# A decoder layer's gate matrix build: slab eviction in runs of four tokens, and GpSimd's products on VectorE

## The chip, the cores and the metric

The kernel runs on one core of one Trainium2 chip. The metric is the device time of one execution in microseconds (us). The engines are named as the profile names them: PE is TensorE (PEld its weight loads), DVE is VectorE, ACT is ScalarE, POOL is GpSimd, SP is SyncE, which here only issues transfers. The five run side by side, each through its own queue of instructions in a fixed order, and wait for each other by semaphores. SBUF is the on-chip memory of 128 partitions, PSUM the memory into which PE writes its results.

## The reference

One decoder layer on 1024 tokens of width 1024: a layer norm, a mixer of eight attention heads with forget gates and four recurrent HGRN2 heads, an output projection, a second norm, and PEER channel mixing over 16384 single-neuron experts. The part around the change is PEER:

```python
q = (xt @ w_q).astype(F32).reshape(T, PEER_HEADS, 2, PEER_HALF)
s = jnp.einsum('thpd,hpnd->thpn', q, sub_keys.astype(F32))
s_top, i_top = lax.top_k(s, PEER_TOPK)
...
best, pos = lax.top_k(cand, PEER_TOPK)
idx = jnp.take_along_axis(cand_idx, pos, axis=-1)
gates = jax.nn.softmax(best, axis=-1)
...
    u = u_tab[idx_b]
    h = jax.nn.gelu(jnp.einsum('td,ted->te', x_b, u), approximate=False) * g_b
    return jnp.einsum('te,ted->td', h, v_tab[idx_b])
```

Each token picks 128 experts (8 heads, 16 each), an expert being a pair (i, j) of 128 by 128, with a gate each.

## The kernel before

The tokens are eight blocks of 128, worked in three groups (256, 512 and 256 tokens). Each group passes through projection, attention and recurrence (`fox`, `hgrn`), output projection with the second norm (`mix_out`), expert selection (`select`, 16 query projections with their top-16 searches on VectorE) and a selection tail.

Then PEER is computed in two ways. Blocks 0, 1, 6 and 7 (`GATHER`) fetch the expert rows of each token by indirect DMAs on GpSimd and multiply them up on VectorE. Blocks 2 to 5 (`DENSE`, 512 tokens) run through all 16384 experts by matrix products, the **dense stage**, which streams both expert tables from memory. For it each dense token needs its gates as a matrix over all experts. `gbuild` makes this **gate matrix**. It runs as a background job: `tick`, called from the loops of the last group's `mix_out` and `select`, lets it advance at set rates, and what is left is drained after `select`, before the dense stage.

How `gbuild` works. A block of 128 tokens goes in 16 groups of 8 tokens (`t8`). For each group four tiles of 128 x 1024 half-precision numbers are made (`per`, line 947; the 128 partitions are the 128 choices of a token, the 1024 columns 8 tokens by 128 values):

- `ohi`: 1 where the choice's i equals the column, always on VectorE; `ohj` the same for j;
- `ah` = `ohi` times the high half of the gate, `al` = `ohi` times its low half.

The constant `GBW` says for each of the four blocks, and for even and odd `t8`, which engine makes `ah`, `al` and `ohj`: `a` is ACT (eight instructions, line 958), `p` GpSimd, `v` VectorE. Tiles have two buffers each. For each token PE multiplies `ohj` by `ah` and by `al` (lines 972 and 974) and adds both in PSUM: 128 by 128 gates, j in the partitions, i in the columns. Four tokens fill one PSUM bank, `pt`, indexed [j, t, i]. ACT copies the bank, scaled, into the **slab** (line 977), a tile of 128 x 128 x 32 numbers indexed [j, i, t] that holds 32 tokens; after eight such evictions SyncE sends it out as 2 MB (line 980, `d_g`). There are 16 slabs and one slab buffer (`slabs = 1`), so the next eviction waits for the landing.

What else runs there, by the names in the rows: `wlo` is the low half of a weight tile, raw minus `whi`, on GpSimd in this stretch (line 213); `cand` are the sums that pairs of scores make (line 833), and `MAX8`, `FIND_INDEX8` and `MATCH_REPLACE8` the top-16 searches on VectorE; `dxt`, `dxh`, `dxl` are the dense tokens, loaded (line 999), transposed by PE and split into halves for the dense stage (lines 273 and 279); `rst`, `rsy`, `g` are tiny operations of norms and gates.

The order on each engine is made by a scheduler when the kernel is built, from the order of the code and estimates of its own; it differs from the order of the code where nothing forbids it.

Of the kernel before, what the change touches and what calls it, by code (L numbers as in the profile page):

```python
# [14 lines left out]
AF = mybir.ActivationFunctionType  # L15
# [43 lines left out]
W0 = 0.71  # L59
BANKS = {"h": 2, "v": 1, "f": 3}  # L60
AHEAD = {('fox', 512): 1, ('mix', 512): 1, ('sel', 512): 1}
GBW = (('apv', 'vvv'), ('apv', 'vvv'), ('apv', 'vvv'), ('vvv', 'vvv'))
LAG = 1
GATHER = (0, 1, 6, 7)
DENSE = (2, 3, 4, 5)
# [6 lines left out]
class Layer:  # L72
# [849 lines left out]
    def gbuild(self, blks, pool):  # L922
        nc, V = self.nc, self.nc.vector
        iota = pool.tile([P, P], F16, name="iota16h", tag="iota16h")
        nc.scalar.activation(iota, self.iota, AF.Copy)
        iv = iota.rearrange("p (m c) -> p m c", c=2).unsqueeze(1).to_broadcast([P, 8, 64, 2])

        def onehots():
            for blk in blks:
                sel = pool.tile([P, 3, P], F32, name="gsl", tag="gsl")  # L930
                nc.sync.dma_start(sel, self.d_sel[blk])
                gs, gh = (pool.tile([P, P], F32, name=n, tag=n, bufs=2) for n in ("gs_", "gh_"))
                g16 = pool.tile([P, P], F16, name="g16", tag="g16")
                pr = pool.tile([P, 4, P, 2], F16, name="gpair", tag="gpair", bufs=2)
                V.tensor_scalar(gs, sel[:, 2], GS, None, op0=ALU.mult)
                V.tensor_copy(g16, gs)
                V.tensor_copy(gh, g16)
                V.tensor_tensor(gs, gs, gh, op=ALU.subtract)
                for n, x in enumerate((sel[:, 0], sel[:, 1], gh, gs)):
                    nc.scalar.activation(pr[:, n], x.unsqueeze(2).to_broadcast([P, P, 2]), AF.Copy)  # L940
                for t8 in range(16):
                    t0 = t8 * 8

                    def per(name, x, n, op, eng=V):
                        t = pool.tile([P, 8, P], F16, name=name, tag=name, bufs=2)
                        y = pr[:, n, t0 : t0 + 8].unsqueeze(2).to_broadcast([P, 8, 64, 2])
                        eng.tensor_tensor(t.rearrange("p t (m c) -> p t m c", c=2), x, y, op=op)
                        return t

                    w = GBW[blks.index(blk)][t8 % 2]  # L950
                    ev = {"v": nc.vector, "p": nc.gpsimd}
                    oi = per("ohi", iv, 0, ALU.is_equal)
                    ov = oi.rearrange("p t (m c) -> p t m c", c=2)
                    oj = per("ohj", iv, 1, ALU.is_equal, ev[w[2]])
                    if w[0] == "a":
                        ah = pool.tile([P, 8, P], F16, name="ah", tag="ah", bufs=2)
                        for t in range(8):
                            nc.scalar.activation(ah[:, t], oi[:, t], AF.Copy, scale=gh[:, t0 + t : t0 + t + 1])
                    else:
                        ah = per("ah", ov, 2, ALU.mult, ev[w[0]])  # L960
                    al = per("al", ov, 3, ALU.mult, ev[w[1]])
                    yield blk, t8, oj, ah, al

        slab = [None]

        def build(blk, t8, oj, ah, al):
            if t8 % 4 == 0:
                slab[0] = pool.tile([P, P, 32], F32, name="slab", tag="slab", bufs=self.slabs)
            for t4 in range(0, 8, 4):
                pt = self.bank("h").rearrange("p (t i) -> p t i", t=4)  # L970
                for t in range(4):
                    nc.tensor.matmul(pt[:, t], oj[:, t4 + t], ah[:, t4 + t], start=True, stop=False,
                                     skip_group_check=True)
                    nc.tensor.matmul(pt[:, t], oj[:, t4 + t], al[:, t4 + t], start=False, stop=True,
                                     skip_group_check=True)
                c = t8 % 4 * 8 + t4
                nc.scalar.activation(slab[0][:, :, c : c + 4].rearrange("p i t -> p t i"), pt, AF.Copy,
                                     scale=1.0 / GS)
            if t8 % 4 == 3:
                self.q("dg").dma_start(self.d_g[DENSE.index(blk) * 4 + t8 // 4], slab[0])  # L980

        oh = onehots()
        cur = next(oh)
        yield 2
        while cur:
            build(*cur)
            cur = next(oh, None)
            yield 2
# [313 lines left out]
```

## Time and profile before

| | us |
|---|---|
| median of three runs (3123.66 to 3131.1) | 3125.99 |
| the profiled execution | 3124.38 |
| its span, first to last instruction | 3122.6 |
| busy in the span: PE / DVE / ACT / POOL | 2629.1 / 2728.4 / 1143.5 / 1725.8 |
| gate matrix build: first product to last landing | about 1242 to 1561 |
| slab evictions on ACT, 128 of them | 127.6 |
| dense stage | about 1561 to the end |

Read a busy time against its own stretch of the program: an engine that is half idle in the whole span can be the one that all others wait for in a part of it. A long mean duration is read against the shortest of the same operation: the difference is time in which the instruction had begun and did not get on. A wait is put down to the event that came last before it ended.

### The profile page before, as it was taken

How to read it: one execution, taken by the hardware profiler on the slowest of the kernel's cores; microseconds unless marked ns; L12 is line 12 of the kernel's file. 1: busy time of each engine (PE TensorE's matmuls, PEld its weight loads, DVE VectorE, ACT ScalarE, POOL GpSimd, SP SyncE). 2: the span in 40 equal slices, each digit the busy share in tenths (PEclk: the TensorE clock that was granted, in tenths of full speed). 3: DMA queues.
4: the chain of work that ended last, by engine and by line, in shares of the span. 5: the costliest groups of instructions: out<-in, count | busy, mean ns of one | idle time of the engine just before them, and what ended most of it. 6: DMA issues, size and time to landing. Idle time of an engine off the chain costs nothing. (4 is left out here: it accounts for less than half of the span.)

```text
span 3122.6 us, 45664 instructions
## 1 busy us (share of the span) xinstructions
PE 2629.1 (84%) x16057; PEld 2161.1 (69%) x16057; DVE 2728.4 (87%) x5549; ACT 1143.5 (37%) x2028; POOL 1725.8 (55%) x1264
## 2 busy tenths in 40 slices
PE   7767799777779767767459899899999999999995
PEld 6767689656657445657347778787778877877874
DVE  8658766588769988989889899899999999999998
ACT  4733222455222433776523223232222323322321
POOL 2343477555756644654036666665467665656652
PEclk9879899888889889878779999999999999999997
DMA  7542599755968857663379999999999999999994
GB/s 272 191 143 81 195 353 318 224 157 169 336 247 297 282 192 268 221 232 149 149 243 366 333 380 359 350 362 367 345 362 371 380 379 357 356 375 337 371 338 159
DMA packets 338662, 887.13 MB, mean 284 GB/s; under 512 B 29912, under 2 KB 124136, under 8 KB 336000
## 3 DMA queue, kind: packets, MB, share of 16 engines
q0 software_dynamic: 147456, 536.94, 47.1%
q1 hardware_dynamic: 185200, 338.38, 31.1%
q10 hardware_dynamic: 5776, 8.90, 0.8%
q8 instruction: 126, 2.06, 0.3%
q14 instruction: 104, 0.85, 0.1%
HBM read 821.67 MB, written 62.42 MB: 283 GB/s over the span
## 5 line engine op out<-in xcount | busy, mean ns | idle before, releaser
L1090 POOL DMA_INDIRECT rows<-in_u,gsel x512 | 689.5, 1347 | 471.5 <-DVE rows L1109 291.7
L1090 POOL DMA_INDIRECT rows<-in_v,gsel x512 | 642.2, 1254 | 417.8 <-DVE ys L1134 261.2
L1109 DVE SCALAR_TENSOR_TENSOR rows<-rows,gx 128x1024 f32<-128x1024 f32 x512 | 633.2, 1285 | 37.9 <-DMA rows<-in_u,gsel 27.0
L1134 DVE SCALAR_TENSOR_TENSOR ys<-rows,sd,ys 128x1024 f32<-128x1024 f32 x381 | 489.7, 1285 | 0.6
L283 PE MATMUL psh<-dxh,uh 128*128 128x512 f32 x1024 | 402.8, 393 | 29.5 <-ACT uh L1016 16.5
L285 PE MATMUL psh<-dxh,ul 128*128 128x512 f32 x1024 | 401.0, 392 | 9.5 <-DVE ul L1017 9.4
L284 PE MATMUL psh<-dxl,uh 128*128 128x512 f32 x1024 | 400.5, 391 | 0.0
L284 PE MATMUL psf<-vl,hh 128*128 128x512 f32 x768 | 310.9, 405 | 44.0 <-DVE vl L1017 43.1
L1016 ACT ACTIVATE vh<-vr 128x512 fp32r<-128x512 f32 x256 | 161.8, 632 | 433.4 <-PE psv L285 402.7
L285 PE MATMUL psf<-vh,hl 128*128 128x512 f32 x768 | 305.8, 398 | 0.0
L283 PE MATMUL psf<-vh,hh 128*128 128x512 f32 x768 | 278.8, 395 | 9.3 <-DVE dy L1049 7.3
L1016 ACT ACTIVATE uh<-ur 128x1024 fp32r<-128x1024 f32 x128 | 136.0, 1062 | 406.2 <-PE psh L284 399.5
L283 PEld LDWEIGHTS psh<-dxh,uh 128*128 128x128 f32 x1024 | 193.5, 189 | 77.2 <-ACT hs L1030 20.5
L285 PEld LDWEIGHTS psh<-dxh,ul 128*128 128x128 f32 x1024 | 193.4, 189 | 50.5 <-DVE ul L1017 10.5
L210 ACT ACTIVATE whi<-wraw 128x1024 fp32r<-128x1024 f32 x130 | 136.5, 1056 | 241.9 <-PE psf L284 62.4
L213 POOL TENSOR_TENSOR wlo<-wraw,whi 128x1024 fp32r<-128x1024 f32 x70 | 172.8, 2474 | 91.7 <-ACT whi L210 89.2
L284 PEld LDWEIGHTS psh<-dxl,uh 128*128 128x128 f32 x1024 | 193.2, 189 | 39.5
L284 PEld LDWEIGHTS psf<-vl,hh 128*128 128x128 f32 x768 | 147.6, 192 | 91.4 <-DVE vl L1017 60.6
L1017 DVE TENSOR_TENSOR vl<-vr,vh 128x512 fp32r<-128x512 f32 x256 | 169.8, 685 | 12.4 <-ACT vh L1016 12.4
L283 PEld LDWEIGHTS psf<-vh,hh 128*128 128x128 f32 x768 | 145.4, 189 | 46.9 <-DVE dy L1049 9.6
L213 DVE TENSOR_TENSOR wlo<-wraw,whi 128x1024 fp32r<-128x1024 f32 x60 | 83.9, 1400 | 106.1 <-ACT whi L210 106.1
L285 PEld LDWEIGHTS psf<-vh,hl 128*128 128x128 f32 x768 | 148.1, 193 | 29.8
(338 smaller groups left out, 6510.4 us busy)
## 6 DMA issues: line engine op xcount, KB each, us to landing
ur<-in_ut SPq DMA_DIRECT2D x128, 512.0 KB
vr<-in_v SPq DMA_DIRECT2D x256, 256.0 KB
d_g<-slab SPq DMA_DIRECT2D x16, 2048.0 KB
gt<-d_g SPq DMA_DIRECT2D x32, 1024.0 KB
wraw<-in_wq SPq DMA_DIRECT2D x48, 512.0 KB
wraw<-in_wt SPq DMA_DIRECT2D x34, 512.0 KB
wraw<-in_wn SPq DMA_DIRECT2D x24, 512.0 KB
wraw<-in_wo SPq DMA_DIRECT2D x24, 512.0 KB
```

Source lines behind the costliest of these rows:

```text
L210: nc.scalar.activation(hi, raw, AF.Copy)
L213: eng.tensor_tensor(lo, raw, hi.bitcast(F32), op=ALU.subtract)
L283: mm(out, lh, rh, start=start, stop=False, **kw)
L284: mm(out, lh, rl, start=False, stop=False, **kw)
L285: mm(out, ll, rh, start=False, stop=stop, **kw)
L1016: nc.scalar.activation(hi, raw, AF.Copy)
L1017: nc.vector.tensor_tensor(lo, raw, hi.bitcast(F32), op=ALU.subtract)
L1090: self.nc.gpsimd.indirect_dma_start(out=t, out_offset=None, in_=tab, in_offset=bass.IndirectOffsetOnAxis(ap=idx, axis=0))
L1109: self.pin(nc.vector.scalar_tensor_tensor(u, u, 1.0, x2, op0=ALU.mult, op1=ALU.mult, accum_out=sd[:, n : n + 1]), "u")
L1134: self.pin(nc.vector.scalar_tensor_tensor(ys, v, h, ys, op0=ALU.mult, op1=ALU.add), "w")
```

## The change

Two edits. In three of the four blocks the `al` tiles of the even `t8` move from GpSimd to VectorE (8 for each block, 24 in all). And the eviction walks the same 512 numbers of a partition in another order: before, token by token, reading PSUM straight through and writing each number 32 numbers (128 bytes) behind the last one in the slab; after, expert by expert, reading the four tokens of one expert 128 numbers (512 bytes) apart in PSUM and writing them as one run of four (16 bytes) in the slab. The slab's contents and its layout stay.

```diff
-GBW = (('apv', 'vvv'), ('apv', 'vvv'), ('apv', 'vvv'), ('vvv', 'vvv'))
+GBW = (('avv', 'vvv'), ('avv', 'vvv'), ('avv', 'vvv'), ('vvv', 'vvv'))
...
-                nc.scalar.activation(slab[0][:, :, c : c + 4].rearrange("p i t -> p t i"), pt, AF.Copy,
+                nc.scalar.activation(slab[0][:, :, c : c + 4], pt.rearrange("p t i -> p i t"), AF.Copy,
                                      scale=1.0 / GS)
```

The scheduler also orders the stretch anew. On the GpSimd queue, at the end of the selection, just ahead of the dense stage's gathers (`in_u`, `in_v`):

```order
-L213 TENSOR_TENSOR wlo<-wraw,whi 128x1024
-L947 TENSOR_TENSOR al<-ohi,gpair 128x1024
-L213 TENSOR_TENSOR wlo<-wraw,whi 128x1024 x2
-L947 TENSOR_TENSOR al<-ohi,gpair 128x1024 x2
-L213 TENSOR_TENSOR wlo<-wraw,whi 128x1024 x2
-L947 TENSOR_TENSOR al<-ohi,gpair 128x1024 x2
+L1090 DMA rows<-in_u,gsel 128x1024 x3
+L213 TENSOR_TENSOR wlo<-wraw,whi 128x1024 x16
 L1090 DMA rows<-in_u,gsel 128x1024 x176
```

Of GpSimd's tensor operations only the `wlo` are left here, the 16 of the selection in a row.

On VectorE, between two top-16 searches of the selection:

```order
 L947 TENSOR_TENSOR ohi<-iota16h,gpair 128x1024
 L796 MAX_INDEX si<-sv,tw_15000 128x8
-L947 TENSOR_TENSOR ohi<-iota16h,gpair 128x1024
+L947 TENSOR_TENSOR ohj<-iota16h,gpair 128x1024
+L947 TENSOR_TENSOR ah<-ohi,gpair 128x1024
+L947 TENSOR_TENSOR al<-ohi,gpair 128x1024
+L947 TENSOR_TENSOR ohi<-iota16h,gpair 128x1024
+L947 TENSOR_TENSOR ohj<-iota16h,gpair 128x1024
+L947 TENSOR_TENSOR al<-ohi,gpair 128x1024
 L792 MAX sv<-s 128x8 x2
```

A whole group with `ah` and `al`, and the next with the `al` that was GpSimd's, now stand ahead of the next search; before, they stood inside it.

On ACT, at the end of the build, with the last slabs and the halves of the dense tokens:

```order
 L273 ACTIVATE dxh<-psf 128x4x128
-L977 ACTIVATE slab<-psh 128x4x128 x14
+L977 ACTIVATE slab<-psh 128x128x4 x16
 L273 ACTIVATE dxh<-psf 128x4x128
-L977 ACTIVATE slab<-psh 128x4x128 x2
+L977 ACTIVATE slab<-psh 128x128x4 x2
+L273 ACTIVATE dxh<-psf 128x4x128
+L977 ACTIVATE slab<-psh 128x128x4 x2
```

The evictions carry their new shape, and two slabs in a row stand without a `dxh` in between; the `dxh` move behind them, among the last slab's evictions. On SyncE the last `dxt` load moves likewise behind one more `d_g` write. From the dense stage on the order of every engine is the same as before.

## Rows read from the trace of the kernel before

**Rows 1.** [...] The first two are `mix_out` of the last group, the third its norm, the fourth the selection, the fifth the drain, the last the dense stage.

```profile
1240.00:1281.00 41.00, 26.01 (x235) 18.65 (x234) 32.01 (x52) 32.65 (x73) 22.57 (x14) 0.79 0.53 179
1281.00:1341.00 60.00, 41.84 (x382) 37.42 (x382) 58.08 (x82) 43.43 (x84) 37.06 (x19) 0.78 0.68 249
1341.00:1374.00 33.00, 20.39 (x151) 16.84 (x149) 26.00 (x28) 25.48 (x53) 16.55 (x7) 0.62 0.73 277
1374.00:1488.00 114.00, 87.72 (x767) 81.10 (x766) 107.75 (x355) 86.08 (x171) 56.60 (x24) 0.88 0.39 147
1488.00:1555.00 67.00, 33.16 (x313) 28.37 (x311) 61.54 (x198) 41.54 (x51) 0.00 (x0) 0.72 0.35 142
...
1640.00:3122.00 1482.00, 1391.71 (x5968) 1125.06 (x5966) 1431.07 (x1934) 425.92 (x626) 911.64 (x675) 0.98 0.95 350
```

**Rows 2.** Groups of instructions from 1240 to 1560 us: line, engine, operation, output and inputs, shapes, count | busy us, mean ns of one | idle us before them and what ended it.

```profile
L977 ACT ACTIVATE slab<-psh 128x512 f32<-128x512 f32 x128 | 127.6, 1075 | 29.4 <-DMA d_g<-slab 19.4 <-PE psh L974 9.4
...
L947 DVE TENSOR_TENSOR ohi<-iota16h,gpair 128x1024 f16<-128x1024 f16 x64 | 69.9, 1096 | 6.3 <-POOL al L947 4.6 <-ACT ah L958 0.8 <-ACT gpair L940 0.6
...
L213 POOL TENSOR_TENSOR wlo<-wraw,whi 128x1024 fp32r<-128x1024 f32 x24 | 61.3, 2564 | 23.8 <-ACT whi L210 23.6
...
L947 DVE TENSOR_TENSOR ohj<-iota16h,gpair 128x1024 f16<-128x1024 f16 x64 | 56.8, 888 | 2.1 <-PE psh L974 1.8
L947 POOL TENSOR_TENSOR al<-ohi,gpair 128x1024 f16<-128x1024 f16 x24 | 54.9, 2286 | 66.4 <-PE psh L974 28.3 <-DVE al L947 14.4 <-DVE ohi L947 12.5
...
L947 DVE TENSOR_TENSOR ah<-ohi,gpair 128x1024 f16<-128x1024 f16 x40 | 29.8, 744 | 12.5 <-PE psh L972 12.3
L947 DVE TENSOR_TENSOR al<-ohi,gpair 128x1024 f16<-128x1024 f16 x40 | 27.2, 681 | 0.0
...
L833 DVE TENSOR_TENSOR cand<-sv 128x48 f32<-128x48 f32 x16 | 11.4, 714 | 0.0
L833 DVE TENSOR_TENSOR cand<-sv 128x64 f32<-128x64 f32 x16 | 11.4, 714 | 0.0
...
L231 DVE SCALAR_TENSOR_TENSOR rsy<-rst,rsy 128x1 f32<-128x1 f32 x3 | 2.2, 724 | 0.0
L229 DVE TENSOR_TENSOR rst<-rsy 128x4 f32<-128x4 f32 x3 | 2.2, 723 | 0.0
```

**Rows 3.** The same operations where nothing disturbs them. The first two rows are from the answers on one tile and give count, shortest, median and longest duration in ns over the whole span; the last is a group from 1240 to 1560 us.

```profile
L947 DVE TENSOR_TENSOR ohi<-iota16h,gpair x64: 665/681/2889, 1242.0 to 1543.2; 128x1024 f16<-128x1024 f16 x64
L833 DVE TENSOR_TENSOR cand<-sv x128: 187/203/2393, 250.5 to 1531.2; 128x64 f32<-128x64 f32 x64, 128x48 f32<-128x48 f32 x64
...
L231 DVE SCALAR_TENSOR_TENSOR rsy<-rst,rsy 128x2 f32<-128x2 f32 x3 | 0.5, 161 | 0.1
```

**Rows 4.** Timeline of GpSimd and VectorE at one place where both work, and of VectorE where GpSimd does not: start, us, engine, line, operation.

```profile
1250.38 1.91 POOL L947 TENSOR_TENSOR al<-ohi,gpair 128x1024 f16<-128x1024 f16 x1
1250.44 2.41 DVE L947 TENSOR_TENSOR ohi<-iota16h,gpair 128x1024 f16<-128x1024 f16 x1
...
1386.62 0.68 DVE L947 TENSOR_TENSOR ah<-ohi,gpair 128x1024 f16<-128x1024 f16 x1
1387.22 0.68 DVE L947 TENSOR_TENSOR al<-ohi,gpair 128x1024 f16<-128x1024 f16 x1
1387.82 0.68 DVE L947 TENSOR_TENSOR ohi<-iota16h,gpair 128x1024 f16<-128x1024 f16 x1
```

**Rows 5.** Who waited for whom from 1240 to 1560 us: us in total, times, longest.

```profile
PE psh L972 <- ACT slab L977: 60.7, 55, 9.0
...
ACT slab L977 <- DMA d_g<-slab: 19.4, 4, 6.4
...
DVE ah L947 <- PE psh L972: 12.3, 4, 6.9
```

**Rows 6.** Timeline of ACT in the drain: the end of one slab and the start of the next, the last pair of evictions, and the first instruction behind the last landing; in brackets the idle time before and what ended it.

```profile
1522.22 1.95 ACT L977 ACTIVATE slab<-psh 128x512 f32<-128x512 f32 x2 [0.20 <-PE psh L974]
1530.56 1.93 ACT L977 ACTIVATE slab<-psh 128x512 f32<-128x512 f32 x2 [6.38 <-DMA d_g<-slab]
...
1552.89 1.92 ACT L977 ACTIVATE slab<-psh 128x512 f32<-128x512 f32 x2
1561.19 1.91 ACT L842 ACTIVATE i<-iota 128x2048 f16<-128x2048 f32 x1 [6.37 <-DMA d_g<-slab]
```

**Rows 7.** Copies with other access, from the answers on one line each: count, shortest, median and longest duration in ns, first and last start. `kn` is a contiguous copy out of PSUM on ACT; `eb` takes 4 numbers; `hTm` writes 32 numbers 132 bytes apart from a contiguous source; `fi` (VectorE) reads SBUF 128 bytes apart and writes contiguously; `sel` (VectorE) is a contiguous copy out of PSUM.

```profile
L977 ACT ACTIVATE slab<-psh x128: 1015/1070/1152, 1249.4 to 1553.7; 128x512 f32<-128x512 f32 x128
L590 ACT ACTIVATE kn<-psh x8: 573/597/597, 131.4 to 1175.5; 128x512 f32<-128x512 f32 x8
L522 ACT ACTIVATE eb<-b x8: 191/206/212, 100.6 to 1083.9; 128x4 f32<-128x4 f32 x8
L1146 ACT ACTIVATE hTm<-hT x4: 257/258/272, 757.7 to 1091.9; 128x32 f32<-128x32 f32 x4
L857 DVE CAST fi<-si x8: 357/368/398, 333.3 to 1599.9; 128x256 f16<-128x256 uint32 x8
L919 DVE COPY sel<-psh x4: 539/550/558, 1141.9 to 1236.8; 128x384 f32<-128x384 f32 x4
```

**Rows 8.** Timeline of SyncE's transfers in the drain.

```profile
1536.60 0.32 SPq L999 DMA_DIRECT2D dxt<-d_x  x1
1539.48 15.68 SPq L980 DMA_DIRECT2D d_g<-slab  x2
```

## The prediction

> **What bounds the kernel now.** The stretch that the change touches comes first. The table of stretches [rows 1] cuts the program at the build of the gate matrix, from about 1240 to 1561 us. In its parts VectorE is busy for 32.0 of 41, 58.1 of 60, 26.0 of 33, 107.8 of 114 and 61.5 of 67 us: 285 of 315, more than any other engine (PE 209, ACT 229, both with pauses everywhere). So VectorE sets the pace here, except in the first part and around 1341 to 1374. Behind the build stands the dense stage, 1482 us at a DMA share of 0.95 with PE and VectorE near full. It starts when the last slab has landed, and none of its instructions change place. What the build gains, the end of the program gains.
>
> How much of VectorE's 285 us is work? The groups of the stretch [rows 2] stand against the same operations undisturbed [rows 3]. An `ohi` takes 681 ns as a rule but 1096 on average; an `ohj` 888; the `cand` sums 714 instead of 203; two groups of tiny operations over 720 ns instead of 161. The timeline shows why [rows 4]: GpSimd starts an `al` at 1250.38 for 1.91 us, VectorE starts an `ohi` 0.06 us later, and it takes 2.41. VectorE stands still while GpSimd works through its tensor operation.
>
> The second chain is the slab's. There is one slab buffer: eight evictions by ACT fill it, 2 MB go out, and only then may the next eviction write. In the last part [rows 6] ACT ends the eighth eviction at 1524.17 and waits 6.38 us for the landing before it starts again at 1530.56, some 15 us per slab (from 1530.56 back by the eight evictions of 1.07 and the 6.38). PE waits 60.7 us for ACT's slab evictions in the stretch, and ACT 19.4 us for landings [rows 5]. VectorE feels this chain as 12.3 us of waiting for PE to read an old `ah`.
>
> **The change part by part.**
>
> *GpSimd's `al` goes away.* Excess of VectorE over its undisturbed durations: 64 x (1096 - 681) = 26.6 us on `ohi`, 64 x (888 - 681) = 13.2 on `ohj`, 40 x (744 - 681) = 2.5 on `ah`, 32 x (714 - 203) = 16.4 on `cand`, 1.7 + 1.7 on the tiny ones in the rows: 62.1 us. GpSimd has two kinds of tensor operations here, 54.9 us of `al` and 61.3 us of `wlo` [rows 2]. Shared by their time, `al` causes 47%, 29.3 us, which go. That no excess belongs to `al` is excluded by the timeline [rows 4]; the other end is what 24 pieces cost if each catches VectorE at 1.73 (2.41 - 0.68), 41 us. I take the share, 29.3. VectorE also waited 4.6 us for a GpSimd `al` before an `ohi` could overwrite its input; that goes too.
>
> *VectorE gets 24 more products.* The same operation on VectorE takes 681 ns, and follow-on ones start every 0.60 to 0.61 us [rows 4]: 24 x 0.61 = 14.6 us on the engine that bounds the stretch, nothing hides it. Each stands in the order right behind its `ohj` and ahead of the next `cand` or `MAX8`, so the top-16 work queues behind it; that is the same 14.6 us, not more.
>
> *`wlo` stays on GpSimd.* Its 24 pieces cost VectorE the other 32.8 us. Relieved of `al`, GpSimd takes each as soon as `whi` is there, and VectorE has more half-precision work to be caught in. At most each piece catches it: 24 x 2.0 = 48 us (the 1.73 of an `al`, plus the 0.28 by which a `wlo` is longer), 15 more than now. At the least nothing changes. I take 4, a quarter, since most are caught already.
>
> *The eviction.* It moves as many elements: 128 instructions of 128x512 at 1075 ns, 127.6 us of ACT. A contiguous copy of this shape out of PSUM takes 597 (`kn`) [rows 7]. The price of the scattered write is seen elsewhere: `hTm` writes 32 elements 132 bytes apart in 258 ns, `eb` 4 elements in 206, which is 1.9 ns for each further element; from `eb` to `kn` each further element of a contiguous output costs 0.8. New are runs of four elements in SBUF and reads 512 bytes apart in PSUM. No row has such a read from PSUM. From SBUF, on VectorE, reads 128 bytes apart cost nothing: `fi` takes 368 ns for 256 elements, 1.44 each, and the contiguous `sel` from PSUM 550 for 384, 1.43 each. So the bounds are 597 (reads free, runs free) and 1075 (the cost moves from write to read), and upward a rival; I take 600, nearest to `fi`. ACT's saving of 128 x 0.475 = 61 us lies beside VectorE's work and counts only where the slab chain is waited for: eight evictions shorten a slab by 3.8 us. Of VectorE's four waits for PE, 12.3 us in all, the longest is 6.9; less 3.8 that leaves 3.1, and the others vanish: 9.2 us gained (0 if the eviction stays as it is, 12.3 at most). At the end, after the last products, ACT has a pair of evictions from 1552.89 [rows 6]: 1 us.
>
> [...]
>
> *Transfers.* Same slab, same 16 transfers. In the new order SyncE issues the last `dxt` load behind one more slab write; now it starts ahead of it, at 1536.60 against 1539.48 [rows 8]. ACT's last evictions are interleaved with `dxh`, which needs this load. It lands after the 6.4 us of the slab write instead of beside it; the last eviction waits for that landing anyway. I put 2 us (0 to 4).
>
> Sum: -29.3 - 4.6 + 14.6 + 4 - 9.2 - 1 + 2 = -23.5 us. The profiled execution took 3124.38 us around a span of 3122.6, which gives 3100.9; the median of the runs lies 1.6 higher at 3125.99, so the forecast is **3102.5 us**.
>
> **The rivals.**
>
> B, the price moves to the read: the eviction stays near 1.07 us. Then -9.2 and -1 fall away, and VectorE, ahead by 15.3 us (29.3 + 4.6 - 14.6 - 4), runs into the slab chain: in the last part a slab's 15 us [rows 6] stand against about 10 of products (16 x 0.61). I let half of the 15.3 be lost: -7.7 + 2 = -5.7, 3120. For it: that no row excludes such a price of a PSUM read. Against it: `fi`.
>
> C, `wlo` takes the place of `al`: +15 instead of +4: 3102.5 + 11 = 3113.5. For it: VectorE is caught within a tenth of a microsecond of GpSimd's start [rows 4]. Against it: 32.8 us over 24 pieces says that two thirds of the `wlo` time is caught now, and why the rest should be is not seen.
>
> D, slower: the strided PSUM read costs more than the strided write did. The slab chain alone then sets the length: 16 landings of 6.4 us and 128 evictions. From the first eviction at 1249.4 [rows 7] to the last landing at 1561.2 [rows 6] it has 312 us now, so it decides from (312 - 102)/128 = 1.64 us per eviction on. At 2.0 (0.6 and three times the present penalty of 0.475) it takes 256 + 102 = 358, +46: 3172. For it no row speaks; none excludes it either, since no row has the access.
>
> E, more than forecast: `al` had the 41 us of its upper bound, all of the 12.3 goes and `wlo` catches no more: -41 - 4.6 + 14.6 - 12.3 + 2 = -41, 3085.
>
> That nothing moves would need another chain as long as VectorE's in the 114 us of selection; PE, at 87.7 of 114 and a granted clock of 0.88, is the nearest. Give it 10 us of the gain, 3112.5.
>
> **How the numbers follow.** The forecast has 0.60, with 3092 to 3110 around it (`wlo` at 0 or near its bound, the waits for PE at 12.3 or at 0). B has 0.15, C and the PE chain 0.13, D 0.06, E 0.06. The range from 3086 to 3122 takes in B and C and leaves out D, half of E and what I have not seen, some 0.15. A measurement tells 0.2%, 6.3 us, from no change: 3119.7. Faster: the forecast, C, E and half of B, less something for the unforeseen, 0.81; the same: the other half of B and part of the unforeseen, 0.11; slower: D and a little, 0.08.
>
> **What would show it.** In the profile after: the `slab` group near 0.60 us (B: 1.07; D: over 1.64); `ohi` and `ohj` means falling from 1096 and 888 to some 850 and 750, with 64 `al` on VectorE at 681 (C: means hardly fall and the `wlo` overlaps grow); VectorE's wait for PE before `ah` nearly gone; the last slab landing near 1537 instead of 1561; the dense stage of unchanged length from there. I am wrong if the last landing moves by less than 10 us although the eviction is short: then VectorE was not the bound. I am also wrong if the landing moves and the end does not.

## The result and the profile after

| | before | after |
|---|---|---|
| median, us (four runs each) | 3128.55 (3123.66 to 3132.01) | 3097.04 (3095.46 to 3099.82) |
| ratio, with its 95% interval | | 0.9908 (0.989 to 0.9926) |
| profiled execution, us | 3124.38 | 3098.22 |
| its span, us | 3122.6 | 3096.5 |
| last slab landed at, us | 1561.2 | 1527.0 |

The change makes the kernel 31.5 us faster by the medians; forecast were 23.5. The windows answer to [rows 1], with the same columns: start and end, length, then for PE, PEld, DVE, ACT and POOL the busy time and the count of instructions, the granted PE clock as a share of full speed, the DMA share and GB/s.

```profile
1240.00:1281.00 41.00, 33.37 (x336) 25.91 (x328) 37.68 (x62) 31.50 (x80) 20.94 (x12) 0.92 0.70 251
1281.00:1341.00 60.00, 36.31 (x357) 32.59 (x357) 54.45 (x101) 42.04 (x103) 16.36 (x11) 0.77 0.80 301
1341.00:1374.00 33.00, 26.59 (x205) 24.18 (x203) 27.49 (x45) 22.13 (x55) 16.09 (x6) 0.79 0.60 215
1374.00:1488.00 114.00, 83.05 (x768) 74.68 (x766) 113.97 (x452) 70.69 (x163) 32.43 (x10) 0.86 0.39 152
1488.00:1555.00 67.00, 38.37 (x239) 32.17 (x238) 48.35 (x124) 24.20 (x38) 3.75 (x3) 0.68 0.52 188
```

In the fourth row VectorE counts 452 instructions in 114 us instead of 355 and pauses for 0.03. By the end of the build everything stands some 34 us earlier, and the last window already holds part of the dense stage. The groups of 1240 to 1560 us answer to [rows 2]:

```profile
L977 ACT ACTIVATE slab<-psh 128x512 f32<-128x512 f32 x128 | 72.1, 598 | 46.5 <-PE psh L974 26.8 <-DMA d_g<-slab 18.8
L213 POOL TENSOR_TENSOR wlo<-wraw,whi 128x1024 fp32r<-128x1024 f32 x24 | 70.2, 2936 | 85.7 <-ACT whi L210 78.6 <-PE psh L974 7.1
...
L947 DVE TENSOR_TENSOR ohi<-iota16h,gpair 128x1024 f16<-128x1024 f16 x64 | 54.9, 860 | 0.8 <-ACT gpair L940 0.5
L947 DVE TENSOR_TENSOR ohj<-iota16h,gpair 128x1024 f16<-128x1024 f16 x64 | 53.4, 835 | 1.6 <-PE psh L974 1.6
L947 DVE TENSOR_TENSOR al<-ohi,gpair 128x1024 f16<-128x1024 f16 x64 | 52.7, 823 | 0.0
...
L947 DVE TENSOR_TENSOR ah<-ohi,gpair 128x1024 f16<-128x1024 f16 x40 | 29.1, 728 | 11.5 <-PE psh L972 11.5
...
L833 DVE TENSOR_TENSOR cand<-sv 128x48 f32<-128x48 f32 x16 | 5.4, 340 | 0.0
...
L833 DVE TENSOR_TENSOR cand<-sv 128x64 f32<-128x64 f32 x16 | 4.3, 270 | 0.0
```

The eviction takes 598 ns instead of 1075. `ohi` falls from 1096 to 860, the `cand` sums from 714 to 340 and 270. What stays long stands beside `wlo`, whose own mean has grown from 2564 to 2936. The waits, as in [rows 5]:

```profile
PE psh L972 <- ACT slab L977: 30.8, 21, 8.5
ACT slab L977 <- PE psh L974: 26.8, 32, 3.8
ACT slab L977 <- DMA d_g<-slab: 18.8, 6, 6.4
...
DVE ah L947 <- PE psh L972: 11.5, 4, 4.2
```

PE waits half as long for evictions, and ACT now waits for PE. VectorE's wait for PE is what it was, 11.5 against 12.3. ACT's end of the build, as in [rows 6], with the landing at the same distance of about 6.4 us from the last eviction's end (1520.64):

```profile
1519.54 1.10 ACT L977 ACTIVATE slab<-psh 128x512 f32<-128x512 f32 x2
1520.49 1.09 ACT L1001 ACTIVATE dy<-dxt 128x1024 f32<-128x1024 f32 x1
1527.01 1.91 ACT L842 ACTIVATE i<-iota 128x2048 f16<-128x2048 f32 x1 [5.43 <-DMA d_g<-slab]
```

**A measure for all kernels.** The *build* is the time from the first `ohi` to the start of line 842's `i`, ACT's first instruction behind it. For the changed kernel the start of the first comes from the answer on the tile `ohi`, that of the last from the answer on line 842 (count, shortest, median and longest duration, first and last start):

```profile
L947 DVE TENSOR_TENSOR ohi<-iota16h,gpair x64: 660/682/2881, 1239.7 to 1510.8; 128x1024 f16<-128x1024 f16 x64
...
L842 ACT ACTIVATE i<-iota x3: 1901/1902/1909, 234.9 to 1527.0; 128x2048 f16<-128x2048 f32 x3
```

1527.0 - 1239.7 = 287.3; before, 1561.2 - 1242.0 = 319.2 [rows 3, 6]. *Held* is VectorE's excess counted piece by piece: each instruction's duration less the shortest of its kind (the same line, operation, shape and tile, whatever the buffer), where that is over 0.15 us, put to the GpSimd operation that it overlaps most. One profile each, in us:

| kernel | time / before (95%) | build | VectorE busy / idle in it | held by `al` / `wlo` |
|---|---|---|---|---|
| before | 1 | 319.2 | 284.9 / 34.3 | 33.0 / 36.2 |
| e1 eviction alone | 0.9991 (0.9979 to 1.0004) | 316.8 | 283.1 / 33.7 | 31.8 / 36.1 |
| e2 products alone | 0.9933 (0.9913 to 0.9952) | 297.4 | 259.3 / 38.1 | 0 / 27.8 |
| after | 0.9908 (0.989 to 0.9926) | 287.3 | 264.3 / 23.0 | 0 / 34.5 |
| e9 after, again | 0.9895 (0.9868 to 0.9922) | 288.8 | 260.8 / 28.0 | 0 / 30.7 |
| e3 48 `al` on GpSimd | 1.0086 (1.0064 to 1.0109) | 342.3 | 298.5 / 43.7 | 67.7 / 29.5 |
| e4 runs of two | 0.9891 (0.9873 to 0.9909) | 288.3 | 261.1 / 27.2 | 0 / 31.2 |
| e5 eight `wlo` on VectorE | 0.9905 (0.9879 to 0.9931) | 287.7 | 260.2 / 27.5 | 0 / 21.3 |
| e6 eight `ah` on ACT | 0.9889 (0.9865 to 0.9912) | 286.9 | 254.2 / 32.7 | 0 / 28.7 |
| e10 the same again | 0.9878 (0.9853 to 0.9903) | 286.7 | 256.1 / 30.6 | 0 / 30.8 |
| e7 24 `ah` on ACT | 0.9947 (0.9929 to 0.9966) | 306.6 | 245.8 / 60.8 | 0 / 26.9 |
| e8 quarter of the slab sent | 0.9877 (0.9853 to 0.9901) | 276.7 | 257.8 / 18.9 | 0 / 28.4 |
| e11 two slabs of half size | 0.9943 (0.9923 to 0.9963) | 289.9 | 263.3 / 26.5 | 0 / 34.7 |
| e12 e11 and e6 | 0.9944 (0.9921 to 0.9967) | 281.5 | 258.4 / 23.1 | 0 / 34.7 |

e1 to e4 ran beside a kernel before of 3126.82 us, e5 to e8 and e9 to e12 on chips where it took 3159.03 and 3154.02; there the first `ohi` starts some 30 us later, so builds and ratios are compared and not times. The three builds of the changed dataflow with a short eviction (after, e9, e4) lie within 1.5 us of each other: a smaller difference between single builds says nothing. How a build divides is less certain still: in the changed kernel's two profiles the busy time differs by 3.5 us and the idle time by 5.0.

Within the build VectorE, ACT and GpSimd work in e1 in the order of the kernel before, and in e2, e4 and e9 in that of the changed kernel. So before and e1, and e2, e4 and the changed kernel, differ by the eviction alone; the new order comes with the 24 products. In the other experiments the order differs too, most in e3, e7, e8, e11 and e12.

### The profile page after: what moved, and what is told of

Same layout as the page of the kernel before. It is cut to its first block, busy times and chain, and to the rows that moved or that the text cites. A ratio compares the mean times of both kernels' runs of the same rounds, so it can differ in the third digit from the quotient of the medians.

```text
span 3096.5 us, 45624 instructions
## 1 busy us (share of the span) xinstructions
PE 2614.4 (84%) x16057; PEld 2150.2 (69%) x16057; DVE 2707.3 (87%) x5573; ACT 1097.2 (35%) x2028; POOL 1678.8 (54%) x1240
## 4 chain that ended last, share of the span: by engine, by line
DVE 40%; PE 36%; issue 11%; DMA 6%; ACT 4%; POOL 3%; SPq 0%; DVEq 0%; POOLq 0%; ACTq 0%
DVE ys L1134 8%; DVE rows L1109 6%; PE psf L284 6%; PE psf L285 5%; PE psf L283 5%; PE psh L285 4%; PE psh L283 4%; PE psh L284 4%; DMA rows<-in_v,gsel 2%; POOL rows L1090 2%; DVE dy L1049 2%; DVE vl L1017 1%; DVE ohj L947 1%; DVE tw L793 1%; DVE al L947 1%
## 5 line engine op out<-in xcount | busy, mean ns | idle before, releaser
L213 POOL TENSOR_TENSOR wlo<-wraw,whi 128x1024 fp32r<-128x1024 f32 x70 | 181.8, 2603 | 154.1 <-ACT whi L210 145.7
```

Source lines behind the costliest of these rows:

```text
L213: eng.tensor_tensor(lo, raw, hi.bitcast(F32), op=ALU.subtract)
```

## The experiments

**The two halves.** e1 is the changed kernel with the `GBW` of before, e2 the changed kernel with the eviction of before.

```diff
 e1
-GBW = (('avv', 'vvv'), ('avv', 'vvv'), ('avv', 'vvv'), ('vvv', 'vvv'))
+GBW = (('apv', 'vvv'), ('apv', 'vvv'), ('apv', 'vvv'), ('vvv', 'vvv'))
 e2
-    nc.scalar.activation(slab[0][:, :, c : c + 4], pt.rearrange("p t i -> p i t"), AF.Copy,
+    nc.scalar.activation(slab[0][:, :, c : c + 4].rearrange("p i t -> p t i"), pt, AF.Copy,
```

> The new eviction alone, with GpSimd keeping its 24 `al`. Theory (VectorE sets the pace and stands still beside GpSimd's products): evictions at 0.60 us, but VectorE stays busy for some 285 us of the build with about 33 us of excess beside `al`; only its waits for PE shrink, by 0 to 13 us. Time 8 us under the kernel before (0 to 13). Rival (the gain of the change is the shorter slab chain, the products don't matter): some 30 us under the kernel before.

> The 24 `al` on VectorE alone, with the eviction of before at 1.07 us. Theory: VectorE's excess beside `al` is gone and its busy time falls to some 264 us, but the slab chain (128 x 1.07 + 16 landings of 6.4 us) now holds it back for part of that, and its waits for PE grow from about 12 us to 20 or more. Time 20 us under the kernel before (8 to 30). Rival (the gain is the slab chain): within 5 us of the kernel before. Second rival (the halves simply add): what this kernel and the eviction alone gain sums to the 31 us of both; by the theory the sum comes out under 31, because each half alone is stopped by the other chain.

e1 took 3123.63 us, 3.2 under the kernel before where 8 (0 to 13) were expected, and the interval holds no change. Its evictions are as short as the changed kernel's (group, stretch of the build):

```profile
L977 ACT ACTIVATE slab<-psh 128x512 f32<-128x512 f32 x128 | 72.7, 597 | 54.5 <-PE psh L974 34.1 <-DMA d_g<-slab 20.0
L947 DVE TENSOR_TENSOR ohi<-iota16h,gpair 128x1024 f16<-128x1024 f16 x64 | 67.6, 1061 | 7.2 <-POOL al L947 5.8 <-ACT gpair L940 1.3
```

55 us of ACT's time are gone and VectorE's standstill is as before: a shorter eviction alone is worth next to nothing. The first rival falls. e2 took 3103.67, 23.2 under: the products, with the order that comes with them, carry the change. Its slab and VectorE's waits (answers on line 977 and on waits):

```profile
L977 ACT ACTIVATE slab<-psh x128: 1007/1075/1153, 1244.6 to 1530.4; 128x512 f32<-128x512 f32 x128
...
  DMA d_g<-slab: 21.0, 7
```

```profile
DVE ah L947 <- PE psh L972: 15.2, 5, 4.0
...
DVE ohj L947 <- PE psh L974: 4.4, 8, 1.6
```

Do the halves add? By the times it can't be told: the ratios' gains are 0.0009 and 0.0067 against 0.0092 with an interval of 0.0018 either way. By the builds they don't: 2.4 + 21.8 = 24.2 against 31.9. On top of the products the short eviction is worth 10.1 us of build, alone 2.4. In e2 VectorE has less work than before but idles 38.1 us; with the short eviction it idles 23.0, and 28.0 in e9.

**Dose.** e3 puts 24 more `al` on GpSimd.

```diff
-GBW = (('avv', 'vvv'), ('avv', 'vvv'), ('avv', 'vvv'), ('vvv', 'vvv'))
+GBW = (('apv', 'vpv'), ('apv', 'vpv'), ('apv', 'vpv'), ('vvv', 'vvv'))
```

> The new eviction, and the `al` of the odd `t8` of three blocks on GpSimd as well, 48 instead of 24 (before) or none (after). Theory: each `al` on GpSimd costs VectorE some 1.4 us of standstill and 0.2 of waiting and saves it 0.6, about 1 us net; so some 24 us over the kernel with the new eviction alone and 47 over the changed kernel, the `al` excess near 66 us. Rival (GpSimd's products run beside VectorE's work at no price, and the change gained by the slab chain): 15 us or more under the kernel with the new eviction alone, since VectorE has 24 products fewer.

3153.72 us, 30.1 over e1: VectorE has 24 products fewer and the kernel is slower, 1.25 us for each (about 1 was expected). 42 of the 48 `al` hold an instruction of VectorE, in e1 20 of 24. Of VectorE's groups:

```profile
L947 DVE TENSOR_TENSOR ohj<-iota16h,gpair 128x1024 f16<-128x1024 f16 x64 | 80.0, 1249 | 2.9 <-PE psh L974 2.8
L947 DVE TENSOR_TENSOR ohi<-iota16h,gpair 128x1024 f16<-128x1024 f16 x64 | 65.1, 1023 | 13.3 <-POOL al L947 10.1 <-ACT ah L958 1.6 <-ACT gpair L940 1.5
```

The work adds up: from e1 VectorE's busy time rises by 15.4, and 35.9 more held by `al`, 6.6 less by `wlo` and 24 products of 0.6 fewer make 14.9. The other 10 us are idle, 4.3 of them waits for `al` (10.1 against 5.8). This balance rests on the held instructions one by one, not on the order. With e1, e2 and this, that GpSimd's `al` hold VectorE is shown.

**Where the eviction's price lies.** e4 writes runs of two tokens.

```diff
-    nc.scalar.activation(slab[0][:, :, c : c + 4], pt.rearrange("p t i -> p i t"), AF.Copy,
+    nc.scalar.activation(slab[0][:, :, c : c + 4].rearrange("p i (a t) -> p a i t", a=2),
+                         pt.rearrange("p (a t) i -> p a i t", a=2), AF.Copy,
```

> The changed kernel, but the eviction writes runs of two tokens (8 bytes) instead of four: for each pair of tokens it walks the 128 experts. If the price is one for each run that does not follow the one before, (1075 - 598)/(512 - 128) = 1.24 ns each: 598 + 128 x 1.24 = 757 ns an eviction. If two numbers in a row are enough: 600. If only a full run of four is free: 1075. Theory for the time: ACT is not the bound, so at 757 ns some 2 us over the changed kernel (0 to 5), although ACT works 20 us more. Rival (the slab chain sets the pace): 8 evictions x 16 slabs x 0.159 = 20 us over.

```profile
L977 ACT ACTIVATE slab<-psh x128: 582/619/675, 1248.1 to 1525.3; 128x512 f32<-128x512 f32 x128
```

The mean is 621 ns, neither 757 nor 1075: two numbers in a row are nearly enough. A price of 1.24 ns for each broken run is refuted. The time, 0.9891 of the kernel before, can't be told from the changed kernel's 0.9908.

**GpSimd's other products.** e5 gives the eight `wlo` of the output projection to VectorE.

```diff
-WDIV = {..., "m2": 1, "s2": 1}
+WDIV = {..., "m2": 0, "s2": 1}
```

> The changed kernel, and the eight `wlo` of the last group's output projection on VectorE instead of GpSimd. Theory (any GpSimd tensor operation holds VectorE's half-precision products): these eight hold VectorE for 15.6 us in the changed kernel; on VectorE each takes 1.22 us undisturbed, 9.8 in all, so the build ends 5.8 us earlier (3 to 8), and VectorE's excess beside `wlo` falls from 34.5 to about 19. Rival (the stand-still is not GpSimd's doing, only put down to it): VectorE has 9.8 us more work, 10 us slower.

The standstill beside `wlo` fell to 21.3, near the 19 expected, but the build is 287.7, no shorter than the changed kernel's, so the 5.8 didn't come. The rival's 10 us didn't come either: 9.8 us of added work on VectorE cost nothing. The expectation went by the one profile in which `wlo` hold VectorE for 34.5; from e9, with 30.7, the exchange is even, 9.4 us of standstill for 9.8 of work, and the builds differ by 1.1.

**VectorE's work against the slab loop.** e6 and e10 are one kernel, e7 goes further, e8 shortens the landing, e11 hides it, e12 is e11 with e6's edit. e9 is the changed kernel, for comparison.

```diff
 e6, e10, e12: GBW's last block
-('vvv', 'vvv')
+('avv', 'vvv')
 e7: also the second and third block
-('avv', 'vvv')
+('avv', 'avv')
 e8
-    self.q("dg").dma_start(self.d_g[DENSE.index(blk) * 4 + t8 // 4], slab[0])
+    self.q("dg").dma_start(self.d_g[DENSE.index(blk) * 4 + t8 // 4][:, :32], slab[0][:, :32])
...
-    self.d_g[:, :, g * JG : (g + 1) * JG, :]
+    self.d_g[:, :, g % 8 * JG : (g % 8 + 1) * JG, :]
 e11, e12 (d_g, gt and the index c follow)
-    if t8 % 4 == 0: slab[0] = pool.tile([P, P, 32], ..., bufs=1)
+    if t8 % 2 == 0: slab[0] = pool.tile([P, P, 16], ..., bufs=2)
```

> The changed kernel, and the eight even `ah` of the last block on ACT instead of VectorE. Theory (VectorE's work is the bound, ACT has room since the eviction is short): 8 x 0.61 = 4.9 us faster (2 to 6); VectorE's busy time in the build falls by as much, ACT's rises by 8 x 8 x 0.39 = 25 us. Rival (ACT's evictions and the slab chain set the pace of the drain): no change or slower, since eight small instructions now stand ahead of evictions.

> As the one before, and the odd `ah` of the second and third block on ACT too: 24 `ah` more on ACT than in the changed kernel, 24 left for VectorE... 48 of 64 in all on ACT. Theory: VectorE has 24 x 0.61 = 14.6 us less; ACT's busy time up to the last landing goes from some 195 us of 287 to 270, so ACT becomes the second bound and gives part back: 5 to 15 us faster. Rival (ACT is the bound from here): VectorE waits for `ah` tiles and the time is within 3 us of the changed kernel or above it.

(16 `ah` are left for VectorE there, not 24.)

> The changed kernel, but of each slab only the first quarter of the experts is sent out (0.5 MB instead of 2), and the dense stage reads that quarter four times: the gates of the other three quarters are left out. A landing takes some 1.6 us instead of 6.4. Theory (VectorE's work is the bound, the slab chain holds it only here and there): VectorE's 11.5 us of waits for PE shrink by part and the last landing by 4.8: 10 us faster (5 to 16). Rival (the slab chain sets the pace with VectorE): 16 x 4.8 = 77 us less in the chain, 25 us faster or more.

> The changed kernel itself, beside the next three on one chip. 0.9908 of the kernel before, as measured (0.989 to 0.9926); the build 287 us long from the first one-hot to the last landing.

> Again the eight even `ah` of the last block on ACT, now beside the changed kernel on one chip. Theory A (VectorE alone bounds the changed build): 5 us faster. Theory B (since the change VectorE and the loop of PSUM bank, eviction, slab and landing bound it together): within 3 us of the changed kernel, and VectorE's idle time up by what its work went down.

> The changed kernel with slabs of 16 tokens and two of them in turn (the same SBUF), each sent as 1 MB while the next is filled; the dense stage reads the gates in runs of 256 bytes instead of 512. Theory A: the build 5 us shorter at most (part of VectorE's 11.5 us of waits for PE). Theory B: some 10 us shorter, as where only a quarter was sent. Both: the dense stage may lose by the shorter runs, 0 to 20 us, so the time says less than the length of the build.

> Both edits at once: two slabs of 16 tokens and the eight `ah` of the last block on ACT. Theory A: the same 5 us that the `ah` alone gain. Theory B: with the landing hidden, VectorE's work is the bound again and the 4.9 us of the eight `ah` show in the length of the build, on top of what the two slabs gain, though alone they show nothing.

e6 and e10: VectorE's busy time fell by 5 to 10 us, and its idle time rose by 3 to 10; the builds are 286.9 and 286.7 against 287.3 and 288.8. By the builds the 4.9 us did not come, as theory B of e10 has it. The times don't decide it: e10's median lies 4.2 us under that of e9, beside it, which fits theory A as well, but the intervals (around 0.9878 and 0.9895) overlap. That this version beats the changed kernel isn't settled. e7 is slower, 306.6, and the expectation missed: ACT is busy for only 234.4 us of them, so it isn't ACT's sum that binds. VectorE's waits there:

```profile
DVE ohj L947 <- PE psh L974: 15.2, 9, 5.6
DVE ohi L947 <- ACT ah L958: 13.2, 13, 1.7
DVE ah L947 <- PE psh L972: 9.3, 5, 3.1
```

VectorE waits for ACT to have read an `ohi` and for PE to have used an `ohj`. The likely reading is that, with two buffers for each tile, eight small ACT instructions in the loop are late for the next group; no run with more buffers tests it.

e8: build 276.7, 10.6 shorter than the changed kernel's, as the theory had it; ACT's wait for landings fell from 18.8 to 3.9, and VectorE's wait of `ah` for PE isn't among its seven longest any more. e11 hides the landing in another way, and ACT's wait for it fell from 19.5 (e9) to 5.8, but its build is 289.9: theory B expected 10 us less and got none. The scheduler orders e11 anew (the first search starts 147.6 us behind the first `ohi`, in e9 127.2), and e8 as well (131.7), so the one edit brings another with it. e12, from nearly the order of e11, has 281.5: there the eight `ah` on ACT are worth 8.4 us, alone 0.4 to 2.1. That agrees with two bounds that hide each other, but 8.4 is more than the 4.9 us of work taken off VectorE, and the rest isn't explained. By themselves e1 and e2 show it: the short eviction is worth 2.4 us of build in the order of before, and 8.6 (to e9) to 10.1 on top of the products. How much the landing alone costs the changed kernel, e8 and e11 answer differently, and that stays open. In time the half slabs lose: the dense stage is 1575.9 and 1585.9 us long against 1562.5 in e9, with 161240 packets under 512 bytes instead of 29912. The page of e9, then of e11:

```profile
DMA packets 338662, 887.13 MB, mean 284 GB/s; under 512 B 29912, under 2 KB 124136, under 8 KB 336000
```

```profile
DMA packets 406502, 887.13 MB, mean 283 GB/s; under 512 B 161240, under 2 KB 189928, under 8 KB 401792
```

No experiment gave a version that is shown to beat the changed kernel.

## Why the prediction was right, and where its terms were off

*GpSimd's `al` goes away: -29.3 forecast.* Right in mechanism, a little small. Piece by piece `al` held VectorE for 33.0 us, and none of it is left. The share of 47% was right (33.0 of 69.2); the excess that it was taken of was too small, 62.1 us from the groups in the rows against 69.2 piece by piece.

*VectorE's wait for GpSimd's `al`: -4.6.* Right: the wait is gone from the `ohi` group.

*24 products on VectorE: +14.6.* Right: e3's balance closes with 0.6 for each.

*`wlo`: +4.* This term failed, sign and all. In the four profiles of kernels with all `al` on VectorE and nothing else moved (after, e9, e4, e2) `wlo` holds VectorE for 34.5, 30.7, 31.2 and 27.8 us, 31.1 on average, against 36.2 in the kernel before: about -5. Only 15 to 19 of the 24 pieces hold VectorE there, 19 before. The prediction let GpSimd catch VectorE's added products; it did not see that it goes the other way round as well. GpSimd and VectorE in the changed kernel, in the selection:

```profile
1428.31 0.69 DVE L947 TENSOR_TENSOR ah<-ohi,gpair 128x1024 f16<-128x1024 f16 x1
1428.91 0.68 DVE L947 TENSOR_TENSOR al<-ohi,gpair 128x1024 f16<-128x1024 f16 x1
1429.51 0.69 DVE L947 TENSOR_TENSOR ohi<-iota16h,gpair 128x1024 f16<-128x1024 f16 x1
1430.12 0.69 DVE L947 TENSOR_TENSOR ohj<-iota16h,gpair 128x1024 f16<-128x1024 f16 x1
1430.72 0.69 DVE L947 TENSOR_TENSOR al<-ohi,gpair 128x1024 f16<-128x1024 f16 x1
1431.32 0.34 DVE L833 TENSOR_TENSOR cand<-sv 128x64 f32<-128x64 f32 x2
1431.57 0.29 DVE L792 MAX8 sv<-s 128x8 f32<-128x128 f32 x1
...
1433.13 0.28 DVE L796 FIND_INDEX8 pos<-best,tw 128x8 uint32<-128x112 f32 x1
1433.31 0.77 DVE L833 TENSOR_TENSOR cand<-sv 128x64 f32<-128x64 f32 x2
```

```profile
1428.66 5.22 POOL L213 TENSOR_TENSOR wlo<-wraw,whi 128x1024 fp32r<-128x1024 f32 x1 [8.54 <-ACT whi L210]
```

A `wlo` that begins at 1428.66, with products of VectorE back to back, ends at 1433.88, 2.5 us after the last product of the row (1431.41). It took 5.22 us, where the shortest `wlo` takes 2.34, and the products beside it 0.68 to 0.69 each: GpSimd has waited, VectorE has not. At another place it is VectorE that stands:

```profile
1263.24 8.50 POOL L213 TENSOR_TENSOR wlo<-wraw,whi 128x1024 fp32r<-128x1024 f32 x3 [3.82 <-ACT whi L210]
```

```profile
1263.94 2.73 DVE L947 TENSOR_TENSOR ohi<-iota16h,gpair 128x1024 f16<-128x1024 f16 x1
1266.58 2.89 DVE L947 TENSOR_TENSOR ohj<-iota16h,gpair 128x1024 f16<-128x1024 f16 x1
```

Beside these `wlo` the `ohi` and the `ohj` took 2.73 and 2.89 us instead of 0.68. In the build the mean `wlo` went from 2564 to 2936 ns and the longest from 3.65 to 5.22 us; what a `wlo` takes longer beside products that run at 0.68 is not VectorE's time. The two places show that either engine can be the one that stands; what decides which, and that this makes all of the 5 us, is not shown.

*The eviction: 1075 to 600.* Right, 598. Rival B's price of the read did not come, although the read is 512 bytes apart in PSUM: 598 ns against 597 for the contiguous `kn` [rows 7]. Rival B's time is refuted by e2 as well: with the eviction at 1.07 us it gave 5.7 us of gain, and e2 gained 23.2.

*What the shorter eviction is worth: -9.2 and -1.* The size nearly came, the mechanism did not, so it was luck that the two agree. The prediction took VectorE's 12.3 us of waiting before `ah` to shrink by 9.2; in the changed kernel they are 11.5, in e9 12.9, in e4 14.8. What the eviction does is to keep other waits from growing once VectorE runs ahead: from e2 to after the build loses 10.1 us, from before to e1 2.4. Among VectorE's waits in e2 besides `ah` are the 4.4 us of `ohj` shown above, and these:

```profile
DVE dxl L279 <- ACT dxh L273: 3.6, 3, 1.5
DVE res L775 <- PE psf L285: 2.3, 2, 1.3
DVE ohi L947 <- ACT ah L958: 2.1, 2, 1.2
```

In the changed kernel `dxl` waits 1.6 us, `ohj` 1.6, `res` 0.2 and `ohi` not at all for ACT's `ah`: 9.0 us less in sum. That is the half of rival B that came true: VectorE, ahead, runs into ACT and the slab chain.

*The late `dxt` load: +2.* Not seen: in 1504 to 1521 VectorE idles 2.6 us, in pieces of at most 0.8, and the last landing keeps its distance from the last eviction.

*The sum.* Of the build's 31.9 us VectorE's busy time gave 20.6 (284.9 to 264.3) and its idle time 11.3 (34.3 to 23.0); by e9 it is 24.1 and 6.3. The prediction had -29.3 + 14.6 + 4 = -10.7 of the one and -4.6 - 9.2 - 1 + 2 = -12.8 of the other. So it took off too little work, by 10 to 13 us, and too much waiting, by 1.5 to 6.5. Of the missing work 3.7 us are `al`; 5.7 are `wlo` (-1.7 in this profile instead of +4; in e9 -5.5), the term that was furthest off; less 1.3 more beside another GpSimd operation (line 261). Counted so, -33.0 + 14.4 - 1.7 + 1.3 = -19.0 of the 20.6 are accounted for; the other 1.6 or so stay open.

*The marks that were named.* The `slab` group and the landing (1527 instead of 1537) went the forecast's way or further; `ohi` at 860 was forecast at 850. `ohj` at 835 and `al` at 823 are longer than the 750 and 681 forecast, since the same standstill beside `wlo` now falls on them too. VectorE's wait before `ah`, which should have been nearly gone, is not.

*The dense stage "of unchanged length".* The landing moved by 34.2 us, the profiled span by 26.1: the stage from `i` to the end took 1561.4 us before and 1569.5 after. That can't be told from scatter: in the eleven profiles with the same instructions there (before, after, e1 to e7, e9, e10) it lies between 1561.4 and 1571.5, and the changed kernel's second profile has 1562.5. The profiled execution of before happened to be a short one; the medians, 31.5 us apart, agree with the builds.

*The rivals.* C (`wlo` takes the place of `al`) and D (a read dearer than the write was) are refuted by the groups. E had the right direction, for `al` and `wlo`, but the 12.3 us of waits did not go. That VectorE sets the pace of the build, as the prediction's first part says, is true of the kernel before (e1); of the one after it is by the builds of e6 and e10 no longer true of VectorE alone.

## What to carry to other kernels

A GpSimd tensor operation beside a VectorE that sets the pace wasn't free help here (24 `al` held VectorE for 33.0 us; as products on VectorE itself they took 14.4): count what it holds piece by piece, each VectorE instruction's excess against the GpSimd operation that it overlaps, before giving GpSimd work that "costs VectorE nothing". Time saved on an engine off the path (ACT's 55 us of evictions) was worth 2.4 us of build by itself and 8.6 to 10.1 once the bound in front of it was lifted; test such edits together and not only alone. Compare stages inside one profile, not ends: the dense stage, at a DMA share of 0.95 [rows 1], differed by up to 10 us from one profile to the next.

## What the runs showed of the hardware that was not expected

- Not every VectorE instruction was held. In the kernel before, the 20 searches (`MAX8`, `FIND_INDEX8`, `MATCH_REPLACE8`) that started beside a GpSimd `al` took at most 21 ns more than their shortest; above, searches run at 0.28 to 0.29 us while the `wlo` works. Held were tensor operations (an `ohi` took up to 2.89 us, its shortest 0.67 [rows 3]), a cast (`g`, line 936: 2.32 us beside a `wlo`, else 0.23) and even the tiny ones of 161 ns (four beside an `al` took 1.86 to 1.87 us).
- ACT writes to SBUF: single numbers 128 bytes apart 1075 ns for 512 (before, e2), runs of two 621 (e4), runs of four 598 (after), a contiguous copy 597 [rows 7]. Why two in a row are nearly enough no run shows.
- Reading PSUM 512 bytes apart cost ACT nothing that can be seen: 598 against 597 [rows 7].
